# Two weight splits of the unit after the last pair, made behind the down products instead of inside the up products

## Chip, cores, metric

One core of a Trainium2 chip runs the whole program in one launch. The metric is device time in microseconds (us): the kernel before has a median of 1266.85 us over 3 runs (1266.41 to 1267.01).

## What is computed

A trunk of two layers over 512 positions of 1024 float32 channels. Each layer has a token mixer (differential attention in layer 0, chunked band attention in layer 1) and then a mixture of 16 experts. The change touches only the experts:

```python
def grouped_moe(h, router_w, router_bias, w_gate, w_up, w_down):
    ...
    for e in range(N_EXPERTS):
        he = jax.nn.silu(t @ w_gate[e]) * (t @ w_up[e])
        out = out + gates[:, e:e + 1] * (he @ w_down[e])
```

The router gives each position two experts of one group of four, so an expert serves only some of the 512 positions. `w_gate` and `w_up` are 1024x512 for each expert, `w_down` is 512x1024: 6 MB of float32 an expert.

## The kernel before

**Units.** The experts are worked off in 12 units, in an order written out in the program (`UNITS`). A unit is one expert with 128 slots for its positions (a single) or two experts with 64 slots each (a pair). Units 2, 4, 6 and 8 are pairs (`TWO`), the others are singles. The program of one layer's experts is the loop over `e` near the end of the kernel. Step `e` makes the gate products of unit `e` (`half(hgT[e], "mm")`, 24 matmuls on TensorE for a single), turns the hidden rows of unit `e - 1`, makes the up products of unit `e` (`half(hgT[e], "s")`), turns the gathered rows of unit `e + 1` (`t_unit`), makes the down products of unit `e - 1`, and evacuates and scatters their result (`evac_y`, `scatter`).

**Singles and pairs.** A pair multiplies raw float32 weights. A single multiplies three products of parts: `three` takes left-hand part hi with weight part hi, lo with hi, and hi with lo (L1416). The weight parts are made in the kernel: `split_half` (L338, L340) takes half of a loaded 1 MB tile, 128x1024; ScalarE (ACT) copies it to `whi`, VectorE (DVE) subtracts to get `wlo`. Four halves make the weights of one product of 24 matmuls: six matmuls a half. There are 4 buffers each of `whi` and `wlo`, so a fifth half can be split only when TensorE (PE) has used up the first.

**Order of the splits.** `half` takes one split half after the other from `split_q`, issues its six matmuls, and then calls `split_next()`, which splits the next half in the list of weights, whichever product it is for. So the gate products of a unit are interleaved with the splits of its up weights, and its up products with the splits of what comes next. If the next weights in the list are raw ones (a pair follows), `split_next` makes nothing. Behind the down products, a loop fills up:

```python
while len(split_q) < 4 and (open_ or pieces and pieces[0][0] != "raw"):
    split_next()
next_slots(e)
```

Every engine works its own instructions in the order of the program, and waits on semaphores for the others.

**Left-hand side.** `t_unit` of a single calls `t_parts` (L1378 to L1393). For each of two halves of the 1024 channels: PE transposes the gathered rows (L1373), ACT scales four blocks into `hgTf` (L1378), ACT copies to `hgTh` (L1392), DVE subtracts to `hgTl` (L1393). `hgTf` has one buffer, so the second half starts behind the first `hgTl`.

**Loads.** All weight tiles are loaded by SyncE's queue (SP, L60) into three rings of 3, 5 and 4 buffers of 1 MB; a load is issued when the buffer's last user is done and when a place among the transfers under way is free.

**Result.** DVE multiplies the down products with the gate weights into `y` (L1460), and GpSimd (POOL) scatters them with an add to the copy of x in device memory, `xb` (L1293), a pair's rows in two scatters. Scatters wait for each other. Behind the last scatter, that of unit 9, x is loaded back (`load_rows`, L1520), and the last two units are added to it on chip (`total`, L1556). `y` has two buffers.

The change lies in `half` (line 1424) and in the step of a unit that follows a pair, which are units 3, 5, 7 and 9. Units 4, 6 and 8 behind the first three are pairs. Below, g10a and g10b are the first and second 1 MB tile of unit 10's gate weights, u10a and u10b those of its up weights.

Of the kernel before, what the change touches and what calls it, by code (L numbers as in the profile page):

```python
# [87 lines left out]
def trunk_kernel(  # L88
# [18 lines left out]
    def bank(tag, bufs):  # L107
        return psum.tile([128, 512], F32, tag=tag, name=tag, bufs=bufs)
# [221 lines left out]
    def split_half(raw, k, scale=None, eng=V, later=None):  # L330

        s = slice(1024 * k, 1024 * k + 1024)
        hi = wsp.tile([128, 1024], F32R, tag="whi", name="whi")
        lo = wsp.tile([128, 1024], F32R, tag="wlo", name="wlo")
        if scale is not None:
            r3 = raw[:, s].rearrange("p (j f) -> p j f", j=2)
            V.tensor_mul(r3, r3, scale[:, None, 512 * k:512 * k + 512].to_broadcast([128, 2, 512]))  # L337
        A.activation(hi, raw[:, s], AF.Copy)  # L338
        if later is None:
            eng.tensor_sub(lo, raw[:, s], hi.bitcast(F32))  # L340
        else:
            later.append(lambda: eng.tensor_sub(lo, raw[:, s], hi.bitcast(F32)))
        return hi, lo
# [638 lines left out]
    TWO = [u for u in range(NU) if len(UNITS[u]) == 2]  # L982
# [31 lines left out]
    for l in range(2):  # L1014
# [30 lines left out]
        def ring_of(w):  # L1045
            return (ring, T["ring"], T.get("ring2"))[w]

        def pass_on():

            while pieces and pieces[0][0] == "dn":  # L1050
                r = ring_of(pieces.pop(0)[2])
                down_q.append((r, r.take()))

        def split_next(eng=V, later=None):

            if open_:
                r, raw = open_.pop()
                split_q.append(split_half(raw, 1, eng=eng, later=later))
                if later is None:
                    r.done(raw)  # L1060
                else:
                    later.append(lambda: r.done(raw))
                return
            pass_on()
            if pieces and pieces[0][0] == "gu":
                r = ring_of(pieces.pop(0)[2])
                raw = r.take()
                split_q.append(split_half(raw, 0, eng=eng, later=later))
                open_.append((r, raw))

        def raw_next():

            pass_on()
            k, _, w = pieces.pop(0)
            assert k == "raw"
            return ring_of(w), ring_of(w).take()
# [290 lines left out]
        hgT, gps, ups, he, heT = {}, {}, {}, {}, {}  # L1367
# [46 lines left out]
        def three(o, lh, ll, wh, wl, first, last):  # L1414
            for i, (a, b) in enumerate(((lh, wh), (ll, wh), (lh, wl))):
                P.matmul(o, a, b, start=(first and i == 0), stop=(last and i == 2))  # L1416

        def pair(b, lhs, w, first, last):

            for h in range(2):  # L1420
                s = slice(64 * h, 64 * h + 64)
                P.matmul(b[s, :], lhs[:, s], w[h], start=first, stop=last)  # L1422

        def half(lhs, tag):
            b = bank(tag, 2)
            if not isinstance(lhs, tuple):
                for k in range(2):
                    ws = [raw_next() for _ in range(2)]
                    for j in range(4):
                        pair(b, lhs[:, 4 * k + j, :], [w[:, 512 * j:512 * j + 512] for _, w in ws],  # L1430
                             k == 0 and j == 0, k == 1 and j == 3)
                    for r, w in ws:
                        r.done(w)
                return b
            while len(split_q) < 2:
                split_next()
            for k in range(4):
                wh, wl = split_q.pop(0)
                for j in range(2):
                    w = slice(512 * j, 512 * j + 512)  # L1440
                    three(b, lhs[0][:, 2 * k + j, :], lhs[1][:, 2 * k + j, :], wh[:, w], wl[:, w],
                          k == 0 and j == 0, k == 3 and j == 1)
                split_next()
            return b

        def act1(g, pool, tag="th", bufs=2):
# [5 lines left out]
        def act2(t, u, pool):  # L1452
            V.scalar_tensor_tensor(t, t, 0.5, u, op0=OP.mult, op1=OP.mult)  # L1453
            return t
# [135 lines left out]
        for e in range(NU + 1):  # L1590
# [6 lines left out]
            if e < NU:  # L1597
                g = half(hgT[e], "mm")
                if pieces and pieces[0][0] == "gu" and e in TWO:
                    split_next()  # L1600
                    split_next()
                th = act1(g, mp)
# [8 lines left out]
                    V.tensor_sub(lo, f[:, 0:2, :], hi.bitcast(F32))  # L1611
                    heT[e - 1] += [hi, lo]
            if e < NU:
                u = half(hgT[e], "s")
                he[e] = act2(th, u, mp)
            if e + 1 < NU:
                hgT[e + 1] = t_unit(e + 1)
# [103 lines left out]
```

## Time and profile before

| | |
|---|---|
| median of 3 runs | 1266.85 us |
| the profiled execution: its own time | 1263.12 us |
| the profiled execution: span of the core | 1261.3 us |
| PE busy | 1161.3 us, 92% of the span |
| DVE busy | 806.1 us, 64% |
| ACT busy | 604.0 us, 48% |
| weight splits on ACT, L338 (mring and ring) | 119.0 + 107.6 us |
| weight splits on DVE, L340 (mring and ring) | 135.8 + 112.8 us |

A profile shows one execution. Busy time is an average over stretches with different limits, so the table says only that PE is the engine nearest to its limit. What a moved instruction is worth is read in the stretch where it stands, from the wait that ends last there. In rows of the trace, "idle before <-releaser" names what ended an engine's idle time.

### The profile page before, as it was taken

Reading aid. Unit: us, or ns where it says so; the run is one execution under the profiler, and the core shown is the slowest. Engines: PE = TensorE matmul, PEld = TensorE weight load, DVE = VectorE, ACT = ScalarE, POOL = GpSimd, SP = SyncE. Lnnn points to the kernel's source line nnn. Section 1 sums busy time; section 2 is a strip of 40 time slices with the busy share of each in tenths; the row PEclk is TensorE's granted clock in tenths of the full one; section 3 lists DMA queues with packets and bytes.
Section 4 is the critical chain, followed back from the end, with each engine's and each line's share of the span. In section 5 each row is a group of like instructions: output and inputs, shape, how many; then the busy total and the mean of one; then the engine's idle time right before and its main releaser. Section 6 shows DMA issues by size and latency. Waiting matters only on the chain. (4 is left out here: it accounts for less than half of the span.)

```text
span 1261.3 us, 19410 instructions
## 1 busy us (share of the span) xinstructions
PE 1161.3 (92%) x7062; PEld 832.5 (66%) x7062; DVE 806.1 (64%) x1850; ACT 604.0 (48%) x1194; POOL 172.2 (14%) x244
## 2 busy tenths in 40 slices
PE   5999898998988999888999999999998899999988
PEld 1788787776755545535769878788775654544565
DVE  2588778787675536525867787856766654553475
ACT  4445455554364444425855444445335543552482
POOL 3100010000421011112110001010033011111210
PEclk8999999999998999999999999999999899999989
DMA  8686554451466999999934635432536699999984
GB/s 303 218 311 231 187 190 145 150 201 67 167 259 238 399 401 405 412 399 408 349 130 145 233 134 206 169 114 92 225 134 244 238 378 399 405 412 401 405 342 144
DMA packets 84111, 327.57 MB, mean 260 GB/s; under 512 B 10791, under 2 KB 35911, under 8 KB 54312
## 3 DMA queue, kind: packets, MB, share of 16 engines
q1 hardware_dynamic: 73352, 302.33, 61.7%
q0 software_dynamic: 10656, 23.93, 7.1%
q8 instruction: 57, 0.93, 0.3%
q14 instruction: 46, 0.38, 0.1%
HBM read 312.53 MB, written 23.15 MB: 266 GB/s over the span
## 5 line engine op out<-in xcount | busy, mean ns | idle before, releaser
L733 PE MATMUL mm<-whi,hT_lo 128*128 128x256 f32 x704 | 201.0, 286 | 0.0
L733 PE MATMUL mm<-whi,hT_hi 128*128 128x256 f32 x704 | 200.0, 284 | 1.0 <-ACT whi L338 0.8
L733 PE MATMUL mm<-wlo,hT_hi 128*128 128x256 f32 x704 | 199.9, 284 | 0.8 <-DVE wlo L340 0.8
L340 DVE TENSOR_TENSOR wlo<-mring,whi 128x1024 fp32r<-128x1024 f32 x116 | 135.8, 1219 | 27.1 <-ACT whi L338 26.4
L340 DVE TENSOR_TENSOR wlo<-ring,whi 128x1024 fp32r<-128x1024 f32 x93 | 112.8, 1225 | 50.9 <-ACT whi L338 50.5
L338 ACT ACTIVATE whi<-mring 128x1024 fp32r<-128x1024 f32 x116 | 119.0, 1056 | 53.2 <-DMA mring<-in_moe_w_gate_dram 22.0
L733 PEld LDWEIGHTS mm<-wlo,hT_hi 128*128 128x128 f32 x704 | 133.1, 189 | 7.1 <-issue 4.5
L826 ACT ACTIVATE p<-p,st 128x128 f32<-128x128 f32 (+3 forms) x128 | 71.0, 555 | 137.8 <-DVE st L823 137.6
L733 PEld LDWEIGHTS mm<-whi,hT_lo 128*128 128x128 f32 x704 | 133.2, 189 | 5.6 <-issue 4.0
L733 PEld LDWEIGHTS mm<-whi,hT_hi 128*128 128x128 f32 x704 | 133.1, 189 | 5.5 <-issue 1.6
L338 ACT ACTIVATE whi<-ring 128x1024 fp32r<-128x1024 f32 x104 | 107.6, 1050 | 12.1 <-DVE ring L337 5.9
L1378 ACT ACTIVATE hgTf<-tr,mcol 128x128 f32<-128x128 f32 x128 | 48.5, 455 | 101.2 <-PE tr L1373 84.4
L1293 POOL DMA_INDIRECT xb<-y,idx x28 | 56.3, 2011 | 167.8 <-DVE y L1460 92.8
L1416 PE MATMUL mm<-whi,hgTh 128*128 128x512 f32 x128 | 56.8, 444 | 12.1 <-ACT hgTh L1392 11.9
L1422 PE MATMUL s<-mring,hgTw 128*64 128x512 f32 x224 | 61.4, 598 | 6.0 <-DMA mring<-in_moe_w_up_dram 5.9
L823 DVE CUSTOM_DVE_ANT_0 p<-s,T 128x128 f32<-128x128 f32 (+3 forms) x128 | 57.8, 486 | 12.3 <-PE s L818 8.8
L1453 DVE SCALAR_TENSOR_TENSOR th<-th,s 128x512 f32<-128x512 f32 x24 | 16.4, 685 | 76.8 <-PE s L1422 58.9
L1287 POOL DMA_INDIRECT hg<-hs,idx x24 | 26.3, 1094 | 287.5 <-DVE idx L1271 130.4
L674 PE MATMUL mm<-whi,o 128*128 128x512 f32 x192 | 61.9, 404 | 1.7 <-DVE xs L678 1.5
L1416 PE MATMUL s<-wlo,hgTh 128*128 128x512 f32 x128 | 52.1, 407 | 9.3 <-DVE wlo L340 9.3
L1416 PE MATMUL mm<-whi,hgTl 128*128 128x512 f32 x128 | 55.0, 430 | 5.5 <-DVE hgTl L1393 5.5
L1393 DVE TENSOR_TENSOR hgTl<-hgTf,hgTh 128x512 fp32r<-128x512 f32 (+1 forms) x36 | 22.7, 632 | 54.7 <-ACT hgTh L1392 54.6
(367 smaller groups left out, 2514.0 us busy)
## 6 DMA issues: line engine op xcount, KB each, us to landing
mring<-in_moe_w_up_dram SPq DMA_DIRECT2D x54, 1024.0 KB, 17.3
mring<-in_moe_w_gate_dram SPq DMA_DIRECT2D x48, 1024.0 KB, 20.7
mring<-in_moe_w_down_dram SPq DMA_DIRECT2D x42, 1024.0 KB, 20.9
ring<-in_ada_w_dram SPq DMA_DIRECT2D x40, 1024.0 KB, 5.6
ring<-in_moe_w_down_dram SPq DMA_DIRECT2D x22, 1024.0 KB, 19.3
ring<-in_moe_w_gate_dram SPq DMA_DIRECT2D x16, 1024.0 KB, 12.8
ring<-in_a_w_qkv_dram SPq DMA_DIRECT2D x24, 512.0 KB, 5.4
ring<-in_b_w_qkv_dram SPq DMA_DIRECT2D x24, 512.0 KB, 5.4
```

What stands on the lines that cost most here:

```text
L338: A.activation(hi, raw[:, s], AF.Copy)
L340: eng.tensor_sub(lo, raw[:, s], hi.bitcast(F32))
L674: P.matmul(ps, a[:, j, ts_], b[:, w], start=(q == 0 and k == 0), stop=(q == 2 and k == 5))
L733: P.matmul(ps[:, :256], a[:, j, ts_], b[:, w], start=(k == 0), stop=(k == 23))
L823: V.tensor_tensor_reduce(out=p[:, :nk], in0=pst[m][:, :nk], in1=T[:, 512 - nk:], scale=-1.0, scalar=3e38, op0=OP.add, op1=OP.min, accum_ou ...
L826: A.activation(p[:, :nk], p[:, :nk], AF.Exp, scale=-1.0, bias=st_[:, m:m + 1], accum_out=st_[:, 2 + m:3 + m])
L1287: G.indirect_dma_start(out=hgs[e % HG], out_offset=None, in_=hs, in_offset=bass.IndirectOffsetOnAxis(ap=idx[:, e:e + 1], axis=0), bounds_c ...
L1293: G.indirect_dma_start(out=xb, out_offset=bass.IndirectOffsetOnAxis(ap=ix[0:n], axis=0), in_=y[0:n], in_offset=None, bounds_check=S - 1, o ...
L1378: A.activation(f, b[:, 128 * (i % 4):128 * (i % 4) + 128], AF.Identity, scale=mcol[:, l, 3, i:i + 1], bias=mcol[:, l, 2, i:i + 1])
L1393: V.tensor_sub(lo[:, s, :], f[:, r, :], hi[:, s, :].bitcast(F32))
L1416: P.matmul(o, a, b, start=(first and i == 0), stop=(last and i == 2))
L1422: P.matmul(b[s, :], lhs[:, s], w[h], start=first, stop=last)
```

## The change

`half` gets a third argument, `own`. Where it is true, only the first two of the four halves are followed by `split_next()`; the loop behind the down products, which is unchanged, makes the two that are missing. It is true for the up products of a unit that follows a pair.

```diff
-        def half(lhs, tag):
+        def half(lhs, tag, own=False):
...
-                split_next()
+                if k < 2 or not own:
+                    split_next()
...
             if e < NU:
-                u = half(hgT[e], "s")
+                u = half(hgT[e], "s", e - 1 in TWO)
                 he[e] = act2(th, u, mp)
```

In units 3, 5 and 7 a pair follows, `split_next` makes nothing there, and no instruction moves. What moves is in unit 9, once in each layer: the two splits of g10b. On ACT in layer 0, from the tanh of unit 9's gate products on; `mring_5900` is g10a, `mring_5910` is g10b, `ring` is u10a and u10b. Before:

```order
L1448 ACTIVATE th<-mm 128x512
L1411 ACTIVATE heT<-tr 128x512
L338 ACTIVATE whi<-mring_5900 128x1024 x2
L338 ACTIVATE whi<-mring_5910 128x1024 x2
L1378 ACTIVATE hgTf<-tr,mcol 128x128 x4
L1392 ACTIVATE hgTh<-hgTf 128x512
L1378 ACTIVATE hgTf<-tr,mcol 128x128 x4
L1392 ACTIVATE hgTh<-hgTf 128x512
L338 ACTIVATE whi<-ring 128x1024 x4
```

The same place after the change, where lines behind 1443 count one higher:

```order
L1449 ACTIVATE th<-mm 128x512
L1411 ACTIVATE heT<-tr 128x512
L338 ACTIVATE whi<-mring_5900 128x1024 x2
L1378 ACTIVATE hgTf<-tr,mcol 128x128 x4
L1392 ACTIVATE hgTh<-hgTf 128x512
L1378 ACTIVATE hgTf<-tr,mcol 128x128 x4
L1392 ACTIVATE hgTh<-hgTf 128x512
L338 ACTIVATE whi<-mring_5910 128x1024 x2
L338 ACTIVATE whi<-ring 128x1024 x4
```

The two copies of g10b have moved behind the ten instructions that make unit 10's left-hand side, and stand ahead of the copies of u10a and u10b as before. On DVE in the same place, before (`th<-th,s` is the product of gate and up of unit 9, `y` the result rows of the pair 8):

```order
L1449 SCALAR_TENSOR_TENSOR th<-th,mm 128x512
L340 TENSOR_TENSOR wlo<-mring_5900,whi 128x1024 x2
L340 TENSOR_TENSOR wlo<-mring_5910,whi 128x1024 x2
L1453 SCALAR_TENSOR_TENSOR th<-th,s 128x512
L1393 TENSOR_TENSOR hgTl<-hgTf,hgTh 128x512 x2
L1460 SCALAR_TENSOR_TENSOR y<-o,wsl,g_3950 128x512
L1460 SCALAR_TENSOR_TENSOR y<-ada,wsl,g_3950 128x512
L340 TENSOR_TENSOR wlo<-ring,whi 128x1024 x4
```

And after the change:

```order
L1450 SCALAR_TENSOR_TENSOR th<-th,mm 128x512
L340 TENSOR_TENSOR wlo<-mring_5900,whi 128x1024 x2
L1454 SCALAR_TENSOR_TENSOR th<-th,s 128x512
L1393 TENSOR_TENSOR hgTl<-hgTf,hgTh 128x512 x2
L340 TENSOR_TENSOR wlo<-mring_5910,whi 128x1024 x2
L1461 SCALAR_TENSOR_TENSOR y<-o,wsl,g_3950 128x512
L1461 SCALAR_TENSOR_TENSOR y<-ada,wsl,g_3950 128x512
L340 TENSOR_TENSOR wlo<-ring,whi 128x1024 x4
```

The two subtractions of g10b have moved behind `th<-th,s` and both `hgTl`, and stand ahead of the `y` rows. PE's order is the same; its waits are not. From the seventh to the eighteenth matmul of unit 10's gate products, with the semaphores waited for, in the changed kernel:

```order
L1416 MATMUL mm<-whi,hgTh 128x512
L1416 MATMUL mm<-whi,hgTl 128x512
L1416 MATMUL mm<-wlo,hgTh 128x512
L1416 MATMUL mm<-whi,hgTh 128x512
L1416 MATMUL mm<-whi,hgTl 128x512
L1416 MATMUL mm<-wlo,hgTh 128x512
L1416 MATMUL mm<-whi,hgTh 128x512 [waits Activation_49]
L1416 MATMUL mm<-whi,hgTl 128x512 [waits DVE_49]
L1416 MATMUL mm<-wlo,hgTh 128x512 [waits DVE_49]
L1416 MATMUL mm<-whi,hgTh 128x512
L1416 MATMUL mm<-whi,hgTl 128x512
L1416 MATMUL mm<-wlo,hgTh 128x512
```

The thirteenth and fourteenth have the waits for ACT and DVE in the kernel before too, for the second half of the left-hand side; the wait of the fifteenth for DVE is new, and so are those of the third (DVE), the nineteenth (ACT) and the twenty-first (DVE). SP and POOL issue the same in the same order.

## Rows read from the trace of the kernel before

**Rows 1.** The page's first part, busy time by engine: PE.
```profile
PE 1161.3 (92%) x7062; PEld 832.5 (66%) x7062; DVE 806.1 (64%) x1850; ACT 604.0 (48%) x1194; POOL 172.2 (14%) x244
```
**Rows 2.** Chain that ended last, 1150 to 1262 us (layer 1): start, us, what.
```profile
1174.85 22.84 DMA mring<-in_moe_w_gate_dram
...
1201.23 0.64 ACT hgTh L1392
...
1201.91 8.50 PE mm L1416 x24
...
1223.55 5.49 PE mm L1416 x24
```
**Rows 3.** Timeline of PE: start, us, instruction, count [idle before <-releaser].
```profile
589.86 3.60 PE L1422 MATMUL ada<-mring,heT 128*64 128x512 f32 x16
598.71 0.79 PE L1416 MATMUL mm<-whi,hgTh 128*128 128x512 f32 x1 [5.25 <-ACT hgTh L1392]
...
606.59 0.63 PE L1373 MATMUL tr<-ident,th 128*128 128x128 f32 x4
...
1201.91 0.80 PE L1416 MATMUL mm<-whi,hgTh 128*128 128x512 f32 x1 [4.83 <-ACT hgTh L1392]
...
1210.25 0.63 PE L1373 MATMUL tr<-ident,th 128*128 128x128 f32 x4
```
**Rows 4.** Timeline of ACT, both layers, around the splits of g10a and g10b.
```profile
589.92 2.01 ACT L338 ACTIVATE whi<-mring 128x1024 fp32r<-128x1024 f32 x2 [8.57 <-DMA mring<-in_moe_w_gate_dram]
594.60 2.00 ACT L338 ACTIVATE whi<-mring 128x1024 fp32r<-128x1024 f32 x2 [2.68 <-DMA mring<-in_moe_w_gate_dram]
596.51 1.49 ACT L1378 ACTIVATE hgTf<-tr,mcol 128x128 f32<-128x128 f32 x4
598.03 0.63 ACT L1392 ACTIVATE hgTh<-hgTf 128x512 fp32r<-128x512 f32 x1
599.48 1.51 ACT L1378 ACTIVATE hgTf<-tr,mcol 128x128 f32<-128x128 f32 x4 [0.82 <-DVE hgTl L1393]
...
1193.11 2.01 ACT L338 ACTIVATE whi<-mring 128x1024 fp32r<-128x1024 f32 x2 [8.12 <-DMA mring<-in_moe_w_gate_dram]
1197.80 2.00 ACT L338 ACTIVATE whi<-mring 128x1024 fp32r<-128x1024 f32 x2 [2.68 <-DMA mring<-in_moe_w_gate_dram]
```
**Rows 5.** Timeline of DVE, layer 0, same place.
```profile
591.01 2.36 DVE L340 TENSOR_TENSOR wlo<-mring,whi 128x1024 fp32r<-128x1024 f32 x2 [6.96 <-ACT whi L338]
...
598.69 0.69 DVE L1393 TENSOR_TENSOR hgTl<-hgTf,hgTh 128x512 fp32r<-128x512 f32 x1
...
602.29 0.74 DVE L1460 SCALAR_TENSOR_TENSOR y<-o,wsl,g 128x512 f32<-128x512 f32 x1
```
**Rows 6.** Line L60, 1177 to 1180.5 us: issues of u10a and u10b, layer 1.
```profile
L60 SPq DMA_DIRECT2D ring<-in_moe_w_up_dram x2: 333/333/333, 1177.3 to 1180.1; - x2
...
DMA to landing us min/median/max: 23.4/23.6/23.7
```
**Rows 7.** Busy time by stretch (us, engines with instructions, PEclk, DMA share, GB/s).
```profile
553.00:563.00 10.00, 6.16 (x28) 2.20 (x28) 1.79 (x3) 1.61 (x3) 2.62 (x2) 1.00 1.03 400
...
1202.00:1207.00 5.00, 5.00 (x11) 3.67 (x12) 2.71 (x5) 3.10 (x6) 0.00 (x0) 0.50 1.01 428
```
**Rows 8.** Timelines of DVE and POOL: a run of splits, and a scatter beside it.
```profile
578.82 4.63 DVE L340 TENSOR_TENSOR wlo<-mring,whi 128x1024 fp32r<-128x1024 f32 x4
...
579.19 5.72 POOL L1293 DMA_INDIRECT xb<-y,idx  x1 [18.69 <-DVE y L1460]
```
**Rows 9.** Line L1293, 570 to 660 us: landings of the layer's last four scatters.
```profile
DMA to landing us min/median/max: 8.6/9.8/14.4
```
**Rows 10.** Layer 0: issue of the reload of x, its landings (line L1520), its first use.
```profile
633.16 1.76 SPq L1520 DMA_DIRECT2D xs<-xb  x4
...
DMA to landing us min/median/max: 5.1/6.9/7.6
...
647.72 0.68 DVE L1556 TENSOR_TENSOR xs<-xs,mm 128x512 f32<-128x512 f32 x1
```

## The prediction, made before the changed kernel ran

> **What bounds the kernel now.** The page's first part names the engine nearest its limit: PE, 92% busy [rows 1]. That says only that a gap of PE is likely to cost time. Which gap does is read from the chain of work that ended last. In layer 1 it runs from the load of g10b (22.84 us from issue to landing) over its copies and unit 10's left-hand side on ACT (hgTh, 0.64 us) into the 24 gate products of unit 10, and from there over PE's next products [rows 2]. So whatever shortens the way into those products shortens the whole.
>
> The timeline of PE shows the gap: after the pair's last down products, PE waits 5.25 us in layer 0 and 4.83 us in layer 1, both for hgTh [rows 3]. The timeline of ACT shows why hgTh is late. ACT gets g10a at 589.92 us, copies it for 2.01 us, waits 2.68 us for g10b to land, copies that from 594.60, and only then scales the rows of unit 10 (596.51, 1.49 us) and makes hgTh (598.03, 0.63 us) [rows 4]. PE restarts at 598.71. Neither the rows nor hgTh need g10b: they stand behind it because ACT works in program order. Layer 1 is the same, with first copies at 1193.11 and 1197.80 [rows 4].
>
> The gap has a second price. The first 24 gate products after it take 8.50 us in layer 1, against 5.49 us for the same 24 of the next unit [rows 2]. In 1202 to 1207 us the granted clock was 0.50, the lower of its two levels, after PE had stood idle [rows 7].
>
> **The change, part by part.** In units 3, 5 and 7 nothing moves, so the first three pairs give nothing. In unit 9 of each layer two copies on ACT and two subtractions on DVE move; PE, SP and POOL keep their order, so no load and no scatter is moved past another.
>
> *The gap.* The rows now follow g10a's copies, so hgTh is earlier by the distance of the two pairs of copies: 594.60 - 589.92 = 4.68 us in layer 0, 1197.80 - 1193.11 = 4.69 us in layer 1 [rows 4]. Both are less than the gaps [rows 3], so all of it counts: PE restarts at 598.71 - 4.68 = 594.03 and at 1197.22. What is left of the gaps is 0.57 and 0.14 us.
>
> *The clock.* With no long idle I take PE to stay at its full level, 5.49 / 24 = 0.229 us a matmul [rows 2]. A stretch with idles of a similar kind as are left, 553 to 563 us with 6.16 us busy of 10, kept a granted clock of 1.00 [rows 7].
>
> *The moved splits, now on PE's way.* The gate products need g10b from the thirteenth matmul on. I follow layer 0, every duration from [rows 4, 5]. hgTh of the first half ends at 593.98. DVE's hgTl, 0.69 us, follows to 594.70, and PE's second matmul waits for it: 0.48 us lost. The second rows start 0.10 us after that hgTl (it ended at 599.38, they began at 599.48), take 1.51, and hgTh 0.63: 596.97. The copies of g10b follow, to 597.93 and 598.9, and its subtractions, 1.18 us each by the 2.36 for two, to 599.2 and 600.3. PE would reach the thirteenth matmul at 594.74 + 11 x 0.229 = 597.26 and starts it at 597.95: 0.69 us lost. The fifteenth needs wlo, 599.2 instead of 598.4: 0.81 us lost. The twenty-first comes at 600.6, behind its wlo. So the products take 5.49 + 0.48 + 0.69 + 0.81 = 7.47 us and end at 601.5; before, PE went on at 606.59 [rows 3]. That is 5.1 us earlier. In layer 1 the same steps start from 1197.22 instead of 594.03 and end at 1204.7; before, PE went on at 1210.25 [rows 3]: 5.5 us earlier.
>
> *Behind it.* DVE, at 600.3, has two y rows of 0.74 us and then u10a's subtractions [rows 5]: the first wlo is there at 602.8. PE's third up product, behind four transposes, comes at about 602.4, so 0.45 us go. After that PE needs six matmuls, 1.37 us, for a half, and DVE 1.18, so DVE falls no further behind. ACT wants u10a at 598.9 in layer 0, so at 1202.1 in layer 1, and its load lands at 1177.3 + 23.7 = 1201.0 [rows 6]: in time, by 1 us. The 1 MB tiles behind it follow 2.8 us apart at issue [rows 6], while PE takes about 5.5 us for the two tiles of a product, so the loads stay ahead, but little more than that: the next thing to be late is a load, not an engine.
>
> *Costs taken as nothing.* g10b's ring buffer is given back some 2 us later than before (600.3 against 594.60 + 2.00 and DVE's share, about 598): the buffer is wanted only by the last down tile of unit 11, which waits for a place among the transfers anyway. If that cover were gone it would cost those 2 us at most. The y rows of the pair come earlier than before (600.3 against 602.29 [rows 5]), so nothing waits longer for them.
>
> **The sum.** Layer 0: 5.1 - 0.45 = 4.6 us. Layer 1: 5.5 - 0.45 = 5.1 us. Together 9.7 us. The profiled execution took 1263.12 us (span 1261.3) and would take 1253.4; the median of the runs lies 3.7 us above it, and I take the same 9.7 us from there: 1257.2 us.
>
> **A rule against the trace.** The y rows are scattered by POOL, and right behind them DVE now runs four subtractions without a break. Such a run shows what that does: beside four subtractions of 4.63 us from 578.82 on, a scatter on POOL took 5.72 us, from 579.19 to 1.46 us after their end [rows 8], and the landings of scatters spread from 8.6 to 14.4 us [rows 9]. I take 14.4 for the pair's first scatter and the median, 9.8, for the two behind it. The Trainium skill, page "SBUF — State Buffer", section "Who interferes with whom", says the opposite of a subtraction: a tensor_tensor takes only the read side of the port pair that DVE shares with GpSimd, while descriptors need the write side (it calls this inferred), so the splits should not hold a scatter up. By it all three scatters would land after 9.8 us and the reload of x would have 6 us to spare. By the row it has 1.4, which is why the next part gives it a chance.
>
> **The rivals.**
>
> *The scatters end the layer (slower).* Place: the two scatters of the pair, that of unit 9, the reload of x, the first addition to x. Scatters wait for each other. The first can be issued at about 602.0. With 14.4 + 9.8 + 9.8, and 0.3 between them, the last lands at 636.6, and the reload, 5.1 us for its first tile [rows 10], at 641.7; the first addition comes at 647.72 - 4.6 = 643.1 [rows 10]. So x is there in time by 1.4 us. It decides from three landings that add up to 35.4 us. If each takes 14.4, x is there at 602.0 + 43.2 + 0.6 + 5.1 = 650.9, that is 3.2 us later than before: twice that is 6.4 us slower, 1273.2. For it: the 14.4 has a row. Against: it has to happen three times in a row, and the later two scatters stand beside a DVE with breaks. Chance 0.04; that it takes some of the gain only (1258 to 1264), 0.06.
>
> *The clock falls all the same.* The short idles could act like one. If it falls before the first product, the 24 take what they took before, PE meets no wait for g10b at that pace, and what is left is the shift less the first wait, 4.7 - 0.5 = 4.2 us a layer: 1258.4. If it falls in the middle, what the lower level cost before is paid on top of the waits, 606.59 - 598.71 - 5.49 = 2.4 us [rows 2, 3] and 8.50 - 5.49 = 3.0 us [rows 2], and 9.7 - 5.4 = 4.3 us are left: 1262.6. Against: the first of [rows 7]. Chance 0.10.
>
> *Nothing changes.* If the loads of g10a and g10b landed some 5 us earlier in the timed runs than in the profiled one, there would be no gap to close, and the change, a no-op in six of its eight places, would do nothing: 1266.9. For it: one execution is all that is seen. Against: the gap is nearly the same in both layers, 5.25 and 4.83 us [rows 3]. Chance 0.07.
>
> *More comes back.* If the splits of g10b come in gaps that I counted as lost, up to 1.5 + 0.45 us more in each layer: 1253.3. It takes a DVE that is faster than its rows. Chance 0.03.
>
> **How the numbers follow.** Forecast 0.70; the other chances stand above. The predicted time is the forecast's, 1257.2. The range reaches to the end of the clock's rival, 1262.6, which takes in most of the partial one, and down to half of what more could come back, 1255.0; outside lie no change, slower, and the ends of two others, about 0.15. A measurement of this kernel can tell 0.2% from no change, 2.5 us. Faster by more than that: 0.70 + 0.06 + 0.10 + 0.03 = 0.89. Within: 0.07. Slower: 0.04.
>
> **What would show it.** Right: on PE the wait before unit 10's gate products falls from 5.25 and 4.83 us to about 0.6 and 0.1; the 24 products take about 7.5 us in both layers, with short waits for `whi` and `wlo` of g10b in the middle, and a granted clock of 1.00; on ACT the rows of unit 10 follow g10a's copies at 591.8; the reload of x lands before its first use. Wrong: a granted clock of 0.50 in the gate products; idle time of PE before the first addition to x or of DVE behind the scatters; ACT waiting for u10a or u11's loads by as much as it no longer waits for g10b, in which case the gap has only moved behind.

## Result and profile after

The changed kernel took 1258.30 us (median of 6 runs, 1254.81 to 1260.14), the kernel before 1266.63 us (6 runs beside them, 1265.74 to 1268.34). The ratio is 0.9934, 95% interval 0.9920 to 0.9948: 8.3 us less, between 6.6 and 10.1. The profiled execution of the changed kernel took 1260.14 us, with a span of 1258.3: it is the slowest of its six, and its distance to the profile of before is only 3.0 us. How that fits is worked out below.

The page's first part, busy time by engine, to be read beside [rows 1]:

```profile
PE 1165.3 (93%) x7062; PEld 832.5 (66%) x7062; DVE 804.6 (64%) x1850; ACT 602.6 (48%) x1194; POOL 171.8 (14%) x244
```

Nothing is to be learned from it: no engine has less to do. The timeline of PE, layer 0 and then layer 1, with all the waits that the view names from the pair's down products to those of unit 10 (start, us, instruction, count, idle before <-releaser), answers to [rows 3]:

```profile
590.89 3.65 PE L1422 MATMUL o<-mring,heT 128*64 128x512 f32 x16
594.37 3.60 PE L1422 MATMUL ada<-mring,heT 128*64 128x512 f32 x16
...
598.59 0.50 PE L1416 MATMUL mm<-whi,hgTl 128*128 128x512 f32 x1 [0.18 <-DVE hgTl L1393]
...
601.80 0.50 PE L1416 MATMUL mm<-whi,hgTh 128*128 128x512 f32 x1 [0.42 <-ACT whi L338]
...
603.06 0.50 PE L1416 MATMUL mm<-wlo,hgTh 128*128 128x512 f32 x1 [0.53 <-DVE wlo L340]
...
605.47 0.63 PE L1373 MATMUL tr<-ident,th 128*128 128x128 f32 x4
...
612.63 0.48 PE L1416 MATMUL o<-whi,heTh 128*128 128x512 f32 x1
...
632.31 0.50 PE L1416 MATMUL o<-wlo,heTh 128*128 128x512 f32 x1 [0.17 <-DVE wlo L340]
632.65 1.88 PE L1642 MATMUL o<-mring,heT 128*128 128x512 f32 x4
...
1191.89 3.65 PE L1422 MATMUL o<-mring,heT 128*64 128x512 f32 x16
...
1202.09 0.50 PE L1416 MATMUL mm<-whi,hgTh 128*128 128x512 f32 x1 [0.16 <-ACT whi L338]
...
1203.35 0.51 PE L1416 MATMUL mm<-wlo,hgTh 128*128 128x512 f32 x1 [0.52 <-DVE wlo L340]
...
1205.76 0.63 PE L1373 MATMUL tr<-ident,th 128*128 128x128 f32 x4
...
1212.94 0.48 PE L1416 MATMUL o<-whi,heTh 128*128 128x512 f32 x1
...
1232.90 0.50 PE L1416 MATMUL o<-wlo,heTh 128*128 128x512 f32 x1 [0.17 <-DVE wlo L340]
1233.23 1.88 PE L1642 MATMUL o<-mring,heT 128*128 128x512 f32 x4
```

The waits of 5.25 and 4.83 us for hgTh are gone entirely. In their place stand the short waits in the middle of the products, for `whi` and `wlo` of g10b, in the thirteenth and the fifteenth matmul. The granted clock of the products (columns: stretch; busy time and instructions of PE, PEld, DVE, ACT, POOL; PEclk; DMA share; GB/s) was 1.00 in both layers, where [rows 7] has 0.50, the lower of the two levels:

```profile
594.00:600.00 6.00, 5.82 (x27) 2.48 (x24) 3.65 (x4) 5.15 (x11) 0.00 (x0) 1.00 1.00 369
1199.00:1205.00 6.00, 5.31 (x21) 3.77 (x22) 3.63 (x4) 5.84 (x9) 0.00 (x0) 1.00 1.01 425
```

The timeline of ACT, layer 0, shows why, beside [rows 4], and a line that has nothing like it before, the last one:

```profile
593.75 2.00 ACT L338 ACTIVATE whi<-mring 128x1024 fp32r<-128x1024 f32 x2 [7.86 <-DMA mring<-in_moe_w_gate_dram]
595.66 1.49 ACT L1378 ACTIVATE hgTf<-tr,mcol 128x128 f32<-128x128 f32 x4
597.17 0.63 ACT L1392 ACTIVATE hgTh<-hgTf 128x512 fp32r<-128x512 f32 x1
...
600.70 2.00 ACT L338 ACTIVATE whi<-mring 128x1024 fp32r<-128x1024 f32 x2
...
612.79 2.02 ACT L338 ACTIVATE whi<-mring 128x1024 fp32r<-128x1024 f32 x2 [2.65 <-DMA mring<-in_moe_w_gate_dram]
```

The rows of unit 10 follow g10a's copies without a pause. But at 612.79 ACT has stood still 2.65 us for the load of g11a, 2.99 us in layer 1. The chain that ended last, layer 1, now runs through that load (start, us, what), where in [rows 2] it ran through the load of g10b:

```profile
1189.06 24.22 DMA mring<-in_moe_w_gate_dram
...
1214.36 1.04 ACT whi L338
1215.39 1.40 ACT hgTf L1378 x4
1216.82 0.64 ACT hgTh L1392
...
1230.58 2.28 DVE wlo L340 x2
1232.86 0.04 issue
1232.90 0.50 PE o L1416
```

**Four marks.** To see where time came and went, I follow four instructions of PE that both kernels have, in both layers: the first down product of the pair 8 (L1422, `o<-mring,heT`), the transposes behind unit 10's gate products (L1373, `tr<-ident,th`), the first down product of unit 9 (L1416, `o<-whi,heTh`), which comes behind unit 10's up products, and the first raw down product of unit 10 (L1641, L1642 after), which comes behind unit 11's gate and up products. Three of them in the timeline of PE of the kernel before (the transposes stand in [rows 3]):

```profile
586.38 3.65 PE L1422 MATMUL o<-mring,heT 128*64 128x512 f32 x16
...
613.42 0.48 PE L1416 MATMUL o<-whi,heTh 128*128 128x512 f32 x1
...
632.57 1.88 PE L1641 MATMUL o<-mring,heT 128*128 128x512 f32 x4
...
1190.00 3.65 PE L1422 MATMUL o<-mring,heT 128*64 128x512 f32 x16
...
1217.08 0.48 PE L1416 MATMUL o<-whi,heTh 128*128 128x512 f32 x1
...
1236.23 1.88 PE L1641 MATMUL o<-mring,heT 128*128 128x512 f32 x4
```

Between them lie three stretches: A (the gap and the gate products of unit 10), B (its up products) and C (unit 9's down products, unit 11's gate and up products, and the first down products of unit 10, up to the raw ones). Their lengths, before and after, in us:

| | A | B | C | gain A, B, C | net |
|---|---|---|---|---|---|
| layer 0, before | 20.21 | 6.83 | 19.15 | | |
| layer 0, after | 14.58 | 7.16 | 20.02 | 5.63, -0.33, -0.87 | 4.43 |
| layer 1, before | 20.25 | 6.83 | 19.15 | | |
| layer 1, after | 13.87 | 7.18 | 20.29 | 6.38, -0.35, -1.14 | 4.89 |

Together 9.3 us net, 12.0 gained in A and 2.7 given back. Between layer 0's last mark and layer 1's first nothing of the change stands, and yet the profile of after is 4.5 us late at the first mark of layer 0 (590.89 against 586.38) and 1.9 us late at that of layer 1. There both kernels run the same program; single executions of the changed kernel differ by 5.3 us (1254.81 to 1260.14). So the profiles' own times differ by 3.0 us, the marks by 9.3 and the medians by 8.3.

### The profile page after: what moved, and what is told of

It reads as the page before. It is cut to its first block, busy times and chain, and to the rows that moved or that the text cites. A ratio compares the mean times of both kernels' runs of the same rounds, so it can differ in the third digit from the quotient of the medians.

```text
span 1258.3 us, 19406 instructions
## 1 busy us (share of the span) xinstructions
PE 1165.3 (93%) x7062; PEld 832.5 (66%) x7062; DVE 804.6 (64%) x1850; ACT 602.6 (48%) x1194; POOL 171.8 (14%) x244
## 5 line engine op out<-in xcount | busy, mean ns | idle before, releaser
L1293 POOL DMA_INDIRECT xb<-y,idx x28 | 56.1, 2003 | 164.5 <-DVE y L1461 80.2
L1422 PE MATMUL s<-mring,hgTw 128*64 128x512 f32 x224 | 63.4, 631 | 8.8 <-DMA mring<-in_moe_w_up_dram 8.8
L1416 PE MATMUL s<-wlo,hgTh 128*128 128x512 f32 x128 | 51.8, 405 | 9.9 <-DVE wlo L340 9.6
L1416 PE MATMUL mm<-whi,hgTl 128*128 128x512 f32 x128 | 53.0, 414 | 5.5 <-DVE hgTl L1393 5.5
L736 ACT ACTIVATE raw<-mm 128x256 f32<-128x256 f32 x88 | 32.9, 374 | 51.5 <-PE mm L733 51.3
```

The source lines that it names most:

```text
L736: A.activation(raw[:, t, :], ps[:, :256], AF.Copy)
L1293: G.indirect_dma_start(out=xb, out_offset=bass.IndirectOffsetOnAxis(ap=ix[0:n], axis=0), in_=y[0:n], in_offset=None, bounds_check=S - 1, o ...
```

## Experiments

Every diff is against the changed kernel unless it says otherwise. "Net by the marks" is the sum of the three gains in both layers, taken from the kernel's own profile. The theory at the outset was that of the prediction, with g11a's load added as the new limit behind it. The ratios come from runs of both kernels beside each other; they need not be the quotient of the two medians.

**one_split: only the last of the two splits moved.**

```diff
-                if k < 2 or not own:
+                if k < 3 or not own:
```

> Only the last of the four early splits is deferred; the first split of g10b stays ahead of unit 10's left-hand side on ACT. Theory (what PE waited for was g10b's landing, passed on by ACT's order): ACT still waits for g10b and is only one copy, 0.95 us, earlier, so PE's gap before unit 10's gate products shrinks from 5.25 and 4.83 us to about 4.3 and 3.9, the granted clock still falls, and the kernel gains about 2 us, 1264.7. Rival (what counts is how much split work stands ahead of hgTh): half the work moved, half of the gain, about 4 us, and a gap of about 2.5 us.

Measured: 1264.99 us against 1264.46, ratio 0.9996 (0.9983 to 1.0009). Net by the marks: 0.3 + 1.2 us. One copy of g10b ahead of the rows is enough to keep most of the gap, 4.29 and 3.47 us of 5.25 and 4.83; its line on PE in layer 0:

```profile
601.41 0.80 PE L1416 MATMUL mm<-whi,hgTh 128*128 128x512 f32 x1 [4.29 <-ACT hgTh L1392]
```

The rival asked for half of the gain, about 4 us, and 1.5 came by the marks. So it is no matter of how much ACT copies: what holds the rows up is an instruction that waits for a load.

**sub_late: the two copies stay inside the up products, only DVE's subtractions of g10b move.**

```diff
-                if k < 2 or not own:
-                    split_next()
+                split_next(later=held if own and k > 1 else None)
...
             for r, wd in raws:
                 r.done(wd)
+            while held:
+                held.pop(0)()
...
```

> ACT keeps the order of the kernel before, both copies of g10b ahead of unit 10's left-hand side; only the two subtractions of g10b on DVE stand where the change puts them. Theory (the gap comes from ACT's wait for g10b): the gap before unit 10's gate products stays at 5.25 and 4.83 us to within 0.5, the clock falls, and the time is that of the kernel before, 1264.5 to 1266.6, within 1 us. Rival (DVE's share of the split holds up hgTl and the y rows): a part of the change's gain, 2 us or more.

Measured: ratio 0.9989 (0.9976 to 1.0002). Net by the marks: -0.15 + 0.23 us, and the gap is 5.25 us in layer 0, as before:

```profile
601.79 0.80 PE L1416 MATMUL mm<-whi,hgTh 128*128 128x512 f32 x1 [5.25 <-ACT hgTh L1392]
```

DVE's part of the change is worth nothing by itself; the gain hangs on ACT's copies.

**fill_gap: the kernel before, with matmuls in the gap whose result nobody reads (`keep_busy(5)`, five in the program, ten in the trace).**

```diff
             for r, wd in raws:
                 r.done(wd)
+            if e == PAIR[0] - 1:
+                keep_busy(5)
```

> The order of the kernel before, with five matmuls of the identity with x added behind the down products of the last pair; their result is not used. They fill some 4.4 us of the gap, so PE still waits for hgTh as long, but does not stand idle. Theory (the low clock behind the gap was a cost of its own): the 24 gate products take about 5.5 to 6 us instead of 7.9 and 8.5, and about 5 us are gained, 1262. Rival (the splits of the up weights would have held PE at that pace anyway, so the clock cost nothing): the products wait for splits instead and the time stays at 1266.6.

Measured: ratio 0.9981 (0.9971 to 0.9992). Net by the marks: 1.5 + 1.9 us, all of it in A. The ten matmuls fill the gap up to 0.76 us, hgTh is as late as before (PE's first gate product stands 12.33 us behind the first mark in both kernels, in layer 0), and the granted clock from 600 to 615 us is 1.00. Two windows, of fill_gap and of the kernel before:

```profile
600.00:615.00 15.00, 14.02 (x52) 9.12 (x52) 10.65 (x12) 12.71 (x21) 2.19 (x1) 1.00 1.01 419
```
```profile
599.00:604.00 5.00, 5.00 (x13) 3.66 (x13) 2.71 (x5) 3.28 (x7) 0.03 (x1) 0.57 1.03 419
```

So the clock by itself, with hgTh as late as it was, is worth 3.4 us by the marks, somewhat over a quarter of the 12.0 that A gained in the change. That is less than the 5 us that were expected: at the full clock the 24 products still take 6.4 us in both layers, from the first product to the second mark, and not 5.5 to 6.

**none_early: no split of what follows inside the up products of unit 9.**

```diff
-                if k < 2 or not own:
+                if not own:
```

> All four early splits of unit 9 are deferred, g10a's too, so unit 10's left-hand side waits for no load. Theory: hgTh is there before the down products end, PE meets no gap and no wait in the gate products (5.5 us instead of the 7.5 of the change), but DVE and the landing of g11a, which ACT meets 2.7 us before it lands in the change, take most of it back: 0 to 1.5 us faster than the change, 1257. Rival (what is left of the change's waits is what is left to gain): 2 us a layer, 1254.5.

Measured: 1257.40 us, ratio 0.9940 (0.9925 to 0.9954). Net by the marks: 3.6 + 4.5 us. A gains more than in the change, 7.3 and 7.7 us, and C gives 3.3 and 3.2 back. The wait has gone to unit 11's gate products, one unit later, with the pattern that the change has in unit 10's:

```profile
616.98 0.50 PE L1416 MATMUL mm<-whi,hgTh 128*128 128x512 f32 x1 [0.28 <-ACT hgTh L1392]
617.71 0.50 PE L1416 MATMUL mm<-whi,hgTl 128*128 128x512 f32 x1 [0.22 <-DVE hgTl L1393]
...
620.92 0.50 PE L1416 MATMUL mm<-whi,hgTh 128*128 128x512 f32 x1 [0.40 <-ACT whi L338]
...
622.18 0.50 PE L1416 MATMUL mm<-wlo,hgTh 128*128 128x512 f32 x1 [0.53 <-DVE wlo L340]
```

**change_10: the change, and the same for unit 10, so that g11a's splits move behind unit 11's rows.**

```diff
-                u = half(hgT[e], "s", e - 1 in TWO)
+                u = half(hgT[e], "s", e - 1 in TWO or e == PAIR[0])
```

> The change, and the two splits of g11a in unit 10's up products deferred in the same way. Theory (behind the change the next late thing is g11a's load, which ACT meets 2.7 and 3.0 us early with unit 11's left-hand side queued behind it): what the trace of the change loses between unit 10's up products and the end of unit 11, 0.8 us in layer 0 and 1.1 in layer 1, is not lost, so about 2 us faster than the change in all, 1256. Rival (DVE is the limit there): the loss stays, 1258.

Measured: 1258.51 us against 1267.00, ratio 0.9937 (0.9916 to 0.9959). Net by the marks: 4.3 + 5.3 us. ACT waits for g11a no more, and C still gives back 0.88 and 0.90. I took that for a verdict against the load and for DVE; it was too quick, as thin_d9 shows: the edit takes one cause away and brings another.

**own_10_too: none_early and change_10 at once.**

```diff
-        def half(lhs, tag, own=False):
+        def half(lhs, tag, own=4):
...
-                if k < 2 or not own:
+                if k < own:
...
-                u = half(hgT[e], "s", e - 1 in TWO)
+                u = half(hgT[e], "s", 0 if e - 1 in TWO else 2 if e == PAIR[0] else 4)
```

> As the kernel with none early in unit 9, and in unit 10 too the two splits of g11a are deferred behind unit 11's left-hand side, so that ACT meets g11a's landing with that work done. Theory (g11a's landing holds up unit 11's left-hand side and through it DVE and PE): 1 us a layer faster than with unit 9 alone, 1255. Rival (DVE, busy without a break from g10b's splits to unit 11's end, is the limit whatever the order): as with unit 9 alone, within 0.5 us a layer.

Measured: 1252.13 us against 1264.46, ratio 0.9898 (0.9878 to 0.9917), the fastest of all. Net by the marks: 6.4 + 6.0 us; C gives back 0.87 and 0.88, as in change_10. On ACT six copies now stand behind unit 11's rows, none of which waits for a load:

```profile
613.62 5.80 ACT L338 ACTIVATE whi<-mring 128x1024 fp32r<-128x1024 f32 x6
```

**pool_sub and own_10_pool: one subtraction of u10b on GpSimd, in the change and in own_10_too.**

```diff
-                    split_next()
+                    split_next(G if k == 3 and side else V)
...
-                g = half(hgT[e], "mm")
+                g = half(hgT[e], "mm", side=e == PAIR[0])
```

> The change, with one of the eight subtractions that DVE makes behind unit 10's rows put on GpSimd: that of the second half of u10b, once in each layer. It replaces no work by less; it only takes 1.18 us off DVE (2.36 for two) behind the gate products. Theory (behind the moved splits DVE is what PE waits for, since it goes on there almost without a break and copies on ACT are followed by short waits of PE for wlo): the waits of PE in unit 11's gate products shrink, some 0.5 to 0.9 us a layer come back, about 1257 where the change has 1258.3. Rival (GpSimd is the wrong place: one such subtraction takes about 2.4 us on it elsewhere in this kernel, and it stands behind a scatter in program order): the wlo of that half comes later than DVE's would have, PE waits for it in the up products, and the time is that of the change or up to 1 us a layer more, 1258 to 1260. Told apart by the net gain up to unit 10's up products (6 us at their end in layer 1 in the change) and by what ends PE's waits there.

> own_10_too (g10b's last splits and those of g11b behind the down products of their units) with the second half of u10b subtracted on GpSimd, once in each layer. Theory (DVE is what PE waits for behind unit 10's rows): some 0.5 to 0.9 us a layer below own_10_too, about 1250.5 to 1251. Rival (GpSimd's subtraction of some 2.4 us is later than DVE's, or DVE and GpSimd hold each other up): 1252 to 1254.

Measured: 1279.16 us, ratio 1.0112 (1.0092 to 1.0132), and 1273.60 us, ratio 1.0060 (1.0040 to 1.0079). Both theories missed by some 22 us, and both rivals by some 20. The rows of POOL and the one wait of PE in layer 0 of pool_sub:

```profile
603.79 2.18 POOL L1293 DMA_INDIRECT xb<-y,idx  x1 [15.65 <-DVE y L1461]
612.40 1.56 POOL L1293 DMA_INDIRECT xb<-y,idx  x1 [6.43 <-DMA xb<-y,idx]
613.40 2.93 POOL L340 TENSOR_TENSOR wlo<-ring,whi 128x1024 fp32r<-128x1024 f32 x1
...
616.39 0.79 PE L1416 MATMUL s<-wlo,hgTh 128*128 128x512 f32 x1 [7.32 <-POOL wlo L340]
```

The subtraction stands on POOL behind the pair's second scatter, and that one waits 6.43 us for the first to land. PE waits 7.32 us, its next matmuls start 0.43 us apart and no longer 0.23, and B gives back 9.5 and 10.0 us. The mistake is the same that the change mends, made on another engine: work behind an instruction that waits for a transfer. On DVE's part in C the two runs say nothing.

**skip_one and skip_four: one, or all four, of DVE's subtractions for u10a and u10b left out.**

```diff
...
+        if not low:
+            return hi, hi
         if later is None:
             eng.tensor_sub(lo, raw[:, s], hi.bitcast(F32))
...
-                    split_next()
+                    split_next(low=not (side and k == 3))
```

(skip_four: `low=not side`.)

> The change, with DVE's subtraction for the second half of u10b left out, once in each layer: that half's six up products use the high part of the weights twice, so the low part of an eighth of unit 10's gate and up weights is missing from the result. PE's matmuls are as many and as long. 1.18 us of DVE's time goes, nothing else. Theory (behind the moved splits DVE is what is late): half a microsecond to 0.9 us a layer comes back between unit 10's up products and the end of unit 11's, 1256.5 to 1257.3 where the change has 1258.3. Rival (the load of g11a, which ACT waits 2.65 us for in layer 0 in the change, is late whatever DVE does): the net gain at unit 10's down products is the change's within 0.3 us, and the time is 1258 to 1258.5.

> The change, with all four of DVE's subtractions for u10a and u10b left out in each layer (unit 10's up products use the high part of the weights twice and lack the low part). 4.7 us of DVE's time goes a layer. Theory (DVE is late): the wait of PE's third up product for wlo goes as well, the gate products of unit 11 meet no wait for wlo, and 0.9 to 1.3 us a layer come back: 1255.7 to 1256.5. Rival (the load of g11a decides): only the 0.35 us at the third up product comes back and is lost again at unit 11's gate products, where PE now waits for whi instead of wlo: 1257.8 to 1258.5. Told apart by the net gain at unit 10's down products and at unit 11's, and by what ends PE's waits between them.

Measured: 1257.52 us, ratio 0.9936 (0.9918 to 0.9953), and 1260.24 us, ratio 0.9956 (0.9939 to 0.9974). Net by the marks: 9.5 and 8.2 us. With 1.18 us less on DVE, C gives back 0.67 and 0.01 us, with 4.7 us less 1.63 and 1.65, and with nothing less, in the change, 0.87 and 1.14: what is lost does not fall with DVE's work ahead of g11a. The 0.35 us of B come back in skip_four and are lost in C, as the rival had it (C loses 0.76 and 0.51 us more than in the change); the time is even a little above the rival's 1258.5. DVE ahead of the load is not what is late.

**Lateness of g11a.** Set against the third mark, the time at which ACT begins its first copy of g11a orders all of these runs:

| | layer | copy of g11a | third mark | copy late by | lost in C |
|---|---|---|---|---|---|
| change | 0 | 612.79 | 612.63 | 0.16 | 0.87 |
| change | 1 | 1213.39 | 1212.94 | 0.45 | 1.14 |
| skip_one | 0 | 609.95 | 609.99 | -0.04 | 0.67 |
| skip_one | 1 | 1210.52 | 1211.22 | -0.70 | 0.01 |
| skip_four | 0 | 612.69 | 611.76 | 0.93 | 1.63 |
| skip_four | 1 | 1212.27 | 1211.33 | 0.94 | 1.65 |
| none_early | 0 | 612.86 | 610.23 | 2.63 | 3.33 |
| none_early | 1 | 1213.65 | 1211.20 | 2.45 | 3.16 |

The loss is the lateness plus 0.70 us, to 0.01 us, in all eight. What makes the copy late is the load in seven of them; in skip_one, layer 1, where next to nothing is lost, ACT waits for a buffer that PE frees (1.86 us), as it does in the kernel before. By this the loss should go when the load comes sooner, which was put to a test.

**thin_d9 and own_10_thin: half a tile less to load ahead of g11a, in the change and in own_10_too.**

```diff
+                if a is None:
+                    continue
...
+                return [a[:, 0:1], None] if thin else [a]
...
-                down = [("gu" if h < n_split(u - 1) else "dn", dn(v, h)) for h in range(2) for v in UNITS[u - 1]]
+                down = [("gu" if h < n_split(u - 1) else "dn", dn(v, h, u == 10 and h)) for h in range(2) for v in UNITS[u - 1]]
...
+                    j2 = 0 if e == 10 else j % 2
...
```

> The change, with only half of the second tile of unit 9's down weights loaded, once in each layer: 0.5 MB less in the queue of loads ahead of g11a (the last quarter of those weights is missing from the result, the matmuls read the third quarter in its place and are as many and as long). 1 MB tiles follow each other 2.5 us apart, so g11a lands some 1.25 us earlier. Theory (what is lost behind unit 10's up products is the lateness of g11a's load: in the change, skip_one, skip_four and none_early, in both layers, the loss between the start of unit 9's down products and unit 10's last down products is 0.70 us plus the time from that start to ACT's first copy of g11a, to 0.03 us, and nothing where the copy starts 0.70 us before it): the copy starts some 1.1 and 0.8 us before the down products instead of 0.16 and 0.45 us behind them, the loss falls from 0.87 and 1.15 us to about 0 in both layers, and the net gain over the kernel before rises from 9.4 to about 11.4 us: 1256.3 beside the change's 1258.3. Rival (DVE's run of splits is what is late, whatever the load does): the loss stays at 0.8 to 1.1 us a layer, 1258.0 to 1258.5. Rival two (the place that half a tile gives back goes to other transfers, and g11a lands when it did): no difference anywhere.

> own_10_too with the same half tile left out. There ACT doesn't copy g11a before unit 11's rows are made, and never waits for its load: the 1.2 us a layer that are lost behind the gate products come with six splits in a row on DVE. Theory (with g11a's splits moved, its load is off the path): g11a lands 1.25 us earlier and the net gain stays at 12.4 us within 0.5, so does the time within what can be told. Rival (the load holds something up there too): 1 us a layer comes back, 14.4 us.

Measured by the marks: C in thin_d9 is 19.14 us in both layers, 0.01 us less than before the change, so nothing is given back. The copies of g11a, at 609.32 and 1210.22, stand 1.81 and 2.15 us ahead of the third mark, and ACT waits 0.75 us where it waited 2.65:

```profile
609.32 2.01 ACT L340 ACTIVATE whi<-mring 128x1024 fp32r<-128x1024 f32 x2 [0.75 <-DMA mring<-in_moe_w_gate_dram]
```

In own_10_thin C gives back 0.87 and 0.92 and the net is 12.4, as in own_10_too. So in the change the load of g11a is what C is lost to, and where g11a's splits are moved it is something else of the same size.

The times don't tell it apart: thin_d9 took 1258.85 us, ratio 0.9938 (0.9915 to 0.9961), own_10_thin 1253.87 us, ratio 0.9905 (0.9885 to 0.9926). The net of thin_d9 is 10.0 us and not the 11.4 expected, because A gained 5.46 and 5.19 us there and not 5.63 and 6.38, for a reason that the next section gives. A difference of 0.6 us is less than such runs can show.

## Why the prediction was right, point by point

It said 1257.2 us and got 1258.3, for the reason that it gave: the waits for hgTh went because its rows no longer stand behind the load of g10b. Its terms came out as follows.

*The gap and the products.* By its steps the products end 11.58 us behind ACT's first copy of g10a (601.5 - 589.92). Measured from that copy to the second mark: 605.47 - 593.75 = 11.72 us in layer 0 and 1205.76 - 1194.02 = 11.74 in layer 1; in change_10, skip_one, skip_four and thin_d9, in both layers, it is 11.70 to 11.73. So the whole way through ACT, DVE and PE was right to 0.16 us. The waits for g10b are in it: in layer 0 the fifteenth matmul starts at 603.06, 2.07 us behind the twelfth (600.99), 1.38 more than three matmuls of 0.229 take, where 0.69 + 0.81 = 1.50 were expected. The 24 products by themselves took 7.56 and 6.85 us, where about 7.5 was said for both layers.

*The distance to the loads.* A gained 5.63 and 6.38 us where 5.1 and 5.5 were predicted, because g10a's first copy came 2.86 and 2.13 us behind the first mark (593.75 - 590.89, 1194.02 - 1191.89), and in the profile of before 3.54 and 3.11 us (589.92 - 586.38, 1193.11 - 1190.00). In that execution PE came later against the loads. With the distances of before, A would have gained 20.21 - 3.54 - 11.72 = 4.95 and 20.25 - 3.11 - 11.74 = 5.40 us. The prediction took the one distance that it had seen, and 1.7 us of the net in this profile come from another. Whether that is chance is open: in layer 0 the distance is 3.51 to 3.55 us in the four kernels that keep the first copy of g10b ahead of the rows, and 2.86 to 3.03 in five of the six where only g10a's copies stand there (pool_sub has 3.57); in layer 1 it is 2.49 to 3.16 and 2.01 to 3.35.

*The clock.* It stayed at 1.00 in the products, and its rival fell. The 5.4 us that the rival set down for the lower level are more than fill_gap gives back by removing it, 3.4.

*The up products.* Predicted 0.45 us lost, measured 0.33 and 0.35.

*Behind it: the step that failed.* The prediction said that the loads stay ahead "but little more than that: the next thing to be late is a load, not an engine", and put that at nothing. It was a load, and it cost 0.87 + 1.14 = 2.0 us. That the loads stay ahead did not follow from its own figures: two tiles at 2.8 us take 5.6 us, no less than the 5.5 that it gave PE for a product. By the trace of before, g11a would still have been in time, by some 0.3 us: issued at 583.7 and landed 24.0 us later, at 607.7, that is 17.8 us behind g10a's first copy, and nothing is lost up to 18.2 (the third mark stands 18.88 behind that copy after the change, less the 0.70 above). After the change it came 19.04 us behind it (612.79 - 593.75), in layer 1 19.37 against 17.9. What took the time is to be seen in the DMA queues (queue: packets, MB, share of the 16 engines) of the last half of that stretch, from 10.1 us behind g10a on. The kernel before, 600.0 to 607.7 us, where the first queue is the only one that moves data beside 0.02 MB of code, and the changed one, 603.8 to 612.7:

```profile
q1 hardware_dynamic: 443, 3.22, 100.2%
```
```profile
q1 hardware_dynamic: 471, 3.43, 92.3%
q0 software_dynamic: 47, 0.17, 9.5%
```

The second queue is POOL's, and its only issue there is the pair's first scatter. It takes 9.5% of 8.9 us, 0.85 us, ahead of g11a's landing, and in layer 1 10.5% of 9.2, 0.97 us; before, none of it. DVE's y rows, and the scatter behind them, come earlier after the change: 603.97 - 589.92 = 14.05 us behind g10a's copy before, 605.74 - 593.75 = 11.99 after. In the first 10.1 us, where the scatter of unit 7 and the gather of rows end, this queue took 15.4% before and 18.8% after, 0.34 us more; in layer 1 17.8 and 21.9%, 0.41 us more. The sums, 1.19 and 1.38 us, come close to the growth of the two stretches (19.0 against 17.8 us, 19.3 against 17.9). So most of it is the pair's scatter, which the change has moved in front of a load that is soon waited for. The prediction wrote of the earlier y rows that "nothing waits longer for them" and left out what their transfer would collide with; its "no load and no scatter is moved past another" holds within each queue, not between the two. thin_d9 fits this: there g11a's first copy comes 17.08 and 16.74 us behind g10a's, 1.96 and 2.63 us sooner than in the change and not only the 1.25 of half a tile, and the second queue moves nothing in the last 6.9 and 6.6 us ahead of g11a's landing. Still, that the load decides is shown, and that the scatter makes it late is read from the rows; no run moved the scatter back alone.

The two misses nearly cancel: 1.7 us more in A, 2.0 us lost in C, 9.3 us by the marks where 9.7 were predicted. The timed 8.3 us (6.6 to 10.1) take in both. That the forecast is so near is luck to that extent.

*The scatters.* The prediction gave the pair's first scatter 14.4 us to land, by [rows 8, 9]. It took 8.7, and 2.18 us on POOL beside a run of four subtractions. DVE and POOL, layer 0:

```profile
605.38 4.62 DVE L340 TENSOR_TENSOR wlo<-ring,whi 128x1024 fp32r<-128x1024 f32 x4
```
```profile
605.74 2.18 POOL L1293 DMA_INDIRECT xb<-y,idx  x1 [14.95 <-DVE y L1461]
```

The row of [rows 8] was a scatter of 128 rows, this one has 64; in the kernel before the same scatter had landed after 8.6 us, the least of [rows 9]. What the run of subtractions costs it can be read from skip_four, where DVE makes none of the four:

```profile
605.21 1.46 POOL L1295 DMA_INDIRECT xb<-y,idx  x1 [15.11 <-DVE y L1463]
```

It landed after 7.6 us there, and in layer 1 it took 1.45 us and landed after 7.8. So the run holds this scatter up by some 0.7 us on POOL, far less than the prediction took. The rule of the Trainium skill, page "SBUF — State Buffer", section "Who interferes with whom", as the prediction put it, would have it not held up at all; these rows do not agree. Nor does the scatter of 128 rows, which took 5.72 us in this profile too, from 583.72 to 1.47 us behind the end of a run of four (583.35 + 4.62).

*The rivals.* That the scatters end the layer fell: x was loaded back from 635.03 us on and first used at 647.80. That nothing changes fell with the marks; more than counted came back in A, but from the loads, not from a faster DVE.

## What to carry to other kernels

An engine that works in program order waits for the slowest thing that any of its instructions needs: before weighing how long the work in front of a critical instruction takes, look whether one piece of it waits for a load. one_split shows that one such piece left in place keeps most of the loss, and pool_sub that the same holds behind a scatter. And when a stall of some us is closed, price the next load against the new time, with every transfer that the change moves in front of it. Moving the consumers of g11a's load out of the way brought nothing on top of the change (change_10, 9.5 us by the marks against 9.3); it took moving g10a's as well (own_10_too, 12.4).

## What was not expected

The way from a load's landing through three engines is very stable: 11.70 to 11.74 us in five kernels, both layers. What varies between profiles is when PE gets there (4.5 us at the first mark, up to which before and after run the same program) and where it then stands against the loads (the distance of g10a's copy to that mark, 2.0 to 3.6 us). So a gain that is read from one profile holds for that profile's distance; marks on both sides of the change, and the distance to the load, are needed to compare two.

The six splits in a row that own_10_too has behind unit 11's rows cost 0.87 and 0.88 us, nearly what g11a's load costs in the change. In layer 0 PE falls behind at two places, by 0.55 us at unit 11's third gate product, which waits for the first `wlo` of g11a, and by the rest at the last matmul with `wlo` ahead of the fourth mark; the view names the first:

```profile
615.98 0.50 PE L1416 MATMUL mm<-wlo,hgTh 128*128 128x512 f32 x1 [0.28 <-DVE wlo L340]
```

No run took either away.
